# A planner that writes the instruction order of a transformer block: its model of loads, pauses, banks and delays is changed

## The chip, the cores and the metric

The kernel runs on one core of one Trainium2 chip. The metric is the device time of one execution in microseconds (us), as a median of three runs. PE is TensorE, which multiplies matrices; DVE is VectorE, ACT is ScalarE, POOL is GpSimd; SP is SyncE, which here only hands out DMA transfers. A name with q (SPq) is that engine's queue of such transfers.

## The reference, cut to what matters

One encoder block over 512 tokens of width 1024 in float32: a half-step feed-forward (FFN1), a mixer of two attention groups, and a second half-step feed-forward (FFN2), each between two RMS norms.

```python
x = x + 0.5 * post1(SwiGLU_1(pre1(x)))    # 1024 -> 2 x 2816 -> 1024
z = pre2(x) @ w_in                        # 1024 -> 1952
o_na  = neighbourhood_attention(q, k, v, rpb)     # 8 heads of 64
o_mla = latent_attention(c_q, c_kv, k_rope, ...)  # 8 heads, low rank
x = x + post2(concat(rms(o_na), rms(o_mla)) @ w_out)
x = x + 0.5 * post3(SwiGLU_2(pre3(x)))
```

A float32 product is made of three products: each operand is split into a rounded part ("hi", written by ACT) and the rest ("lo", written by DVE or POOL), and hi*hi, hi*lo and lo*hi are summed in PSUM.

## The kernel before, in words

**FFN1 and FFN2.** The hidden width of 2816 is cut into 22 chunks of 128. Every chunk has a gate and an up weight of 512 KB each. The first chunks (7 in FFN1, 3 in FFN2) are multiplied directly: 24 matmuls of 512 columns for the gate and 24 for the up weight. The others use a Strassen-Winograd scheme with 84 matmuls of 256 columns and sums on DVE and POOL. The results go to a DRAM buffer (gd); the down projection reads them back and goes over the same 22 chunks.

**The start of FFN1 (L588 to L654).** The transposed input comes in eight pieces (`load_xT`), the weights of chunks 0 and 1 as load 0 to load 3 (`load_wx`; 0 gate, 1 up of chunk 0; 2 gate, 3 up of chunk 1). There are three raw buffers: load 3 goes to the buffer of load 0 (L594), so it can start when load 0 has been split. Input rows for the norm come as four tiles of 512 KB (L646); their squares are written to PSUM banks 0 and 1 as scratch (L648), which chunk 2 needs for its sums (L388: chunk c uses banks (4+2c) and (5+2c) modulo 8). Eight small matmuls spread the norm into bank 3. `ident` (64 KB), `g_o` (4 KB) and `tokt` (128 KB) are also loaded here; the last two are used only in the mixer.

**The mixer.** `qk_pair`, `na_pair`, `k_pair`, `mla_pair`, `w_out_a` and `w_out_b` are written out in order; many of their operations read or write half the partitions of a PSUM bank.

**What sets the order.** Nothing is issued as it is written. Class `Plan` records every operation with its dependencies (`add`, `runs`, `touch`) and a reckoned duration. `place` runs a list scheduler over the five engines: at each step the engine that is free first takes the ready operation of best priority. It runs backward (which gives each operation a due time) and forward (with the due times as priority), six rounds in all (`issue`); the forward order with the shortest reckoned span is issued, sorted by reckoned start. The dependencies and semaphores on the chip follow from that order; each engine works through its list in it. Every recorded instruction is issued by L220, so the profile knows all of them by that one line, and they are told apart by engine, shape and tile (m: plain float32 tiles, memr: tiles of split operands). In `place`, an SP operation costs SP 330 ns, and its transfer is added to a line of transfers (`dma`) that can grow without bound.

Of the kernel before, what the change touches and what calls it, by code (L numbers as in the profile page):

```python
# [4 lines left out]

# [1 line left out]

# [5 lines left out]
F32 = mybir.dt.float32  # L13
# [15 lines left out]
NH = 8  # L29
TAIL = 4  # L30

# [12 lines left out]
class Plan:  # L44

    TAIL = {"ACT": 95, "DVE": 75, "POOL": 60, "PE": 176}

    def __init__(self, tc):  # L50
        self.tc, self.ops, self.maps = tc, [], {}
# [12 lines left out]
    @staticmethod  # L64
    def runs(x):

        name, ap = x.tensor.name, [list(d) for d in x.ap]
        kind = name.rsplit("_", 1)[0]
        if kind in ("h1", "h2", "gd0", "gd1"):
            n = math.prod(c for _, c in ap)  # L70
            return [((kind, 0), [(x.offset, x.offset + n)])]
        if kind not in ("m32", "memr", "psum"):
            return []
        pitch, parts = ap[0]
        p0, o = divmod(x.offset, pitch)
        runs = [(o, o + 1)]
        for step, c in sorted(ap[1:], key=lambda d: abs(d[0])):
            if step == 0 or c == 1:
                continue
            lo, hi = runs[0][0], runs[-1][1]  # L80
            if abs(step) <= hi - lo:
                a, b = (0, step * (c - 1))[:: 1 if step > 0 else -1]
                runs = [(lo + a, hi + b)]
            else:
                runs = sorted((a + step * i, b + step * i) for i in range(c) for a, b in runs)
        if kind == "psum":
            runs = sorted({(a // 512 * 512, (b + 511) // 512 * 512) for a, b in runs})
        halves = [i for i in range(2) if p0 < 64 * i + 64 and p0 + parts > 64 * i]
        return [((kind, i), runs) for i in halves]

# [18 lines left out]
    def add(self, eng, op, a, k):  # L109
        is_ap = lambda x: hasattr(x, "ap") and hasattr(x, "offset")  # L110
        outs = [x for x in (*a[:1], k.get("out"), k.get("accum_out")) if x is not None and is_ap(x)]
        ins = [x for x in (*a[1:], *(v for n, v in k.items() if n not in ("out", "accum_out"))) if is_ap(x)]
        n, deps = len(self.ops), set()
        for x in ins:
            for key, runs in self.runs(x):
                for lo, hi in runs:
                    self.touch(n, key, lo, hi, key[0] == "psum", deps)
        for x in outs:
            for key, runs in self.runs(x):
                for lo, hi in runs:  # L120
                    self.touch(n, key, lo, hi, True, deps)
        cols = max(math.prod(c for _, c in list(x.ap)[1:]) for x in outs[:1] + ins)
        kind = lambda x: x.tensor.name.rsplit("_", 1)[0]
        size = math.prod(c for _, c in list(outs[0].ap))
        big = [x for x in ins if math.prod(c for _, c in list(x.ap)[1:]) > 1]
        in_sb = sum(kind(x) != "psum" for x in big)
        tail, lock, dma = self.TAIL.get(eng, 0), False, 0
        if op == "dma_start":
            run = min(list(x.ap)[-1][1] for x in (outs[0], ins[0]))
            dma = 4 * size / (280 if run >= 512 else 230 if run >= 256 else 180 if run >= 128 else 60)  # L130
            busy, tail = (330 if eng == "SP" else 400 if eng == "ACT" else 1000), 0
        elif eng == "PE":
            busy = max(109, (cols + 32) / 2.4)
            tail += cols / 2.4 - busy
        else:
            fix, per = {"ACT": (190, 0.834) if in_sb else (132, 0.872), "DVE": (140, 1.045), "POOL": (90, 1.0)}[eng]
            if ALU.pow in a:
                fix, per = 390, 160
            elif eng == "POOL" and in_sb > 1:
                fix, per = (130, 2.2) if cols > 256 else (300, 1.2)  # L140
            fix += 90 * (AF.Exp in a) + 45 * (op == "scalar_tensor_tensor")
            if k.get("accum_out") is not None:
                fix += 195 if eng == "ACT" else 75
            busy = fix + per * cols - tail
            in_psum = sum(kind(x) == "psum" for x in big + outs)
            lock = in_sb > 1 or in_sb and (eng == "POOL" or not in_psum and eng == "DVE")
        self.ops.append((eng, op, a, k, deps, busy, tail, lock, dma))

    def place(self, prio, back):

        ops, n = self.ops, len(self.ops)
        left, after = self.left[back][:], self.after[back]
        free = dict.fromkeys(self.engines, 0.0)
        ready = {e: [] for e in free}
        soon = {e: [] for e in free}
        est, start = [0.0] * n, [0.0] * n
        lock = dma = idle = warm = 0.0
        for i in range(n):
            if not left[i]:
                heappush(soon[ops[i][0]], (0.0, prio[i], i))  # L160
        done = 0
        while done < n:
            t, e = min((max(free[e], 0.0 if ready[e] else soon[e][0][0]), e) for e in free if ready[e] or soon[e])
            ahead = 0 if e == "PE" or e == "SP" else 250
            while soon[e] and soon[e][0][0] <= t + ahead:
                s, p, i = heappop(soon[e])
                heappush(ready[e], (p, i))
            p, i = heappop(ready[e])
            _, _, _, _, deps, busy, tail, lk, xfer = ops[i]
            s = max(t, est[i])  # L170
            if lk:
                s = max(s, lock)
                lock = s + busy
            if e == "PE" and not back:
                if s > idle + 1900:
                    warm = s + 3400
                if s < warm:
                    busy *= 2 if busy > 110 else 1.2
                idle = s + busy
            free[e] = s + busy  # L180
            if xfer:
                if back:
                    x = max(s + 500, dma)
                    dma = x + xfer
                    end = dma + 1300 + 330
                else:
                    x = max(s + busy + 1300, dma)
                    dma = x + xfer
                    end = dma + 500
            else:  # L190
                end = s + busy + tail
            start[i] = s if not back else -(end if xfer else s + busy)
            done += 1
            for j in after[i]:
                est[j] = max(est[j], s + busy if ops[j][0] == e and not xfer else end + 40)
                left[j] -= 1
                if not left[j]:
                    heappush(soon[ops[j][0]], (est[j], prio[j], j))
            self.span = max(free.values())
        return start  # L200
# [28 lines left out]
def hybrid_block(ctx, tc, A, out):  # L229
# [94 lines left out]
    def load_w(src, n=1024, eng=DVE, raw=None, to=None):  # L324
        raw = fetch(src, n) if raw is None else raw
        hi, lo = to or (his.get()[:, :n], los.get()[:, :n])
        split(hi, lo, raw, eng)
        return hi, lo
# [45 lines left out]
    def ffn(w_gu, w_dn, gpost, on_tile, L, first, resid, mid_tile=None, rs=None):  # L374
# [139 lines left out]
        def down(c, n, w, first, last, hfs=(0, 1)):  # L514
            t = slice(n * P, (n + 1) * P)
            for (a, b) in ((0, 0), (0, 1), (1, 0)):
                for hf in hfs:
                    mm(bank(2 * n + hf), gT[c][a][:, t], w[b][:, hf * 512 : hf * 512 + 512],
                       first and a + b == 0, last and a == 1)
# [10 lines left out]
        for n in range(NT):  # L530
            SP.dma_start(h[n], resid(n))
        for c in range(2, NFC - TAIL):
            w = load_w(w_dn[c * P : (c + 1) * P, :])
# [3 lines left out]
        ws = []  # L537
        for c in range(NFC - TAIL, NFC):
            ws.append(load_w(w_dn[c * P : (c + 1) * P, :], to=last_w if c == NFC - 1 else None))
            load_gT(c)  # L540
        ts, sqs = cut(1024, 2), cut(512, 2, 2048)
        for n in range(NT):
            s = stat.get()
            t = ts.get()
            for hf in range(2):
                c = slice(hf * 512, hf * 512 + 512)
                for i, k in enumerate(range(NFC - TAIL, NFC)):
                    down(k, n, ws[i], False, i == TAIL - 1, (hf,))
                if hf == 0 and mid_tile:
# [650 lines left out]
```

## Time and profile before

| | us |
|---|---|
| median of 3 runs | 966.41 (966.3 to 966.68) |
| the profiled execution, its own time | 969.88 |
| its span, first to last instruction | 968.1 |
| PE busy | 948.5 (98%) |
| DVE busy | 692.8 (72%) |
| ACT busy | 464.5 (48%) |
| POOL busy | 302.0 (31%) |

Busy time is the time in which an engine has at least one instruction under way. The profiled execution is 3.5 us longer than the median run, so differences read in it are carried over to the median and not its absolute time. Its mean granted PE clock is 0.991 of full speed.

### The profile page before, as it was taken

To read this page: it belongs to the slowest core of one execution; us is meant where nothing else is said; L and a number is where in the kernel's file an instruction comes from. 1 tells how busy PE (TensorE), PEld (TensorE's weight loads), DVE (VectorE), ACT (ScalarE), POOL (GpSimd) and SP (SyncE) were. 2 spreads that over 40 slices of the span, in tenths; PEclk is the share of its full clock that TensorE was granted. 3 is DMA by queue.
4 is the path that set the end of the run, shared out by engine and by line. 5 is a ranking of instruction groups with operands and counts; after the bars stand their busy time and mean duration, and the time that the engine had idled before them with its cause. 6 is when DMAs were issued, how large, how long until landed. Compare 5 with 4: busy or idle time off the path is not lost. (4 is left out here: it accounts for less than half of the span.)

```text
span 968.1 us, 15209 instructions
## 1 busy us (share of the span) xinstructions
PE 948.5 (98%) x5878; PEld 851.8 (88%) x5878; DVE 692.8 (72%) x963; ACT 464.5 (48%) x801; POOL 302.0 (31%) x240
## 2 busy tenths in 40 slices
PE   9999999999999999999999989899999999999997
PEld 7788999999888888888988878799999999988885
DVE  4896999998522385567686587998999999742224
ACT  5553454444421362677567765764444444441211
POOL 0002767650000013222351422227777574000000
PEclk9999999999999999999999999999999999999999
DMA  9644334359743446122370112454433436753312
GB/s 288 205 156 131 128 132 145 117 155 306 225 113 96 140 159 131 62 75 45 109 165 1 66 44 88 152 183 136 151 120 110 152 127 217 250 170 109 87 44 87
DMA packets 60905, 130.11 MB, mean 134 GB/s; under 512 B 21920, under 2 KB 22816, under 8 KB 60832
## 3 DMA queue, kind: packets, MB, share of 16 engines
q1 hardware_dynamic: 59248, 126.25, 41.6%
q0 software_dynamic: 1008, 1.84, 1.1%
q10 hardware_dynamic: 576, 1.05, 0.3%
q8 instruction: 46, 0.75, 0.3%
q14 instruction: 27, 0.22, 0.1%
HBM read 109.45 MB, written 17.83 MB: 131 GB/s over the span
## 5 line engine op out<-in xcount | busy, mean ns | idle before, releaser
L220 PE MATMUL psum<-memr 128*128 128x256 f32 (+2 forms) x5520 | 921.9, 327 | 7.7 <-ACT memr L220 3.1
L220 PEld LDWEIGHTS psum<-memr 128*128 128x128 f32 x5520 | 809.6, 191 | 94.8 <-DVE memr L220 7.4
L220 DVE TENSOR_TENSOR memr<-m,memr 128x512 fp32r<-128x512 f32 (+3 forms) x310 | 353.7, 1168 | 144.1 <-ACT memr L220 143.9
L220 POOL TENSOR_TENSOR m<-m 128x512 f32<-128x512 f32 (+3 forms) x193 | 264.5, 1385 | 476.0 <-DVE m L220 368.3
L220 ACT CAST memr<-m 128x512 fp32r<-128x512 f32 (+3 forms) x318 | 259.9, 843 | 297.9 <-PE psum L220 213.5
L220 DVE TENSOR_TENSOR m<-psum,m 128x512 f32<-128x512 f32 (+3 forms) x205 | 119.9, 589 | 36.0 <-ACT m L220 21.7
L220 DVE TENSOR_TENSOR memr<-psum,memr 128x512 fp32r<-128x512 f32 (+3 forms) x116 | 68.0, 603 | 30.7 <-ACT memr L220 29.6
L220 ACT CAST memr<-psum 128x512 fp32r<-128x512 f32 (+3 forms) x124 | 62.4, 524 | 41.6 <-PE psum L220 31.8
L220 DVE TENSOR_TENSOR m<-m 128x512 f32<-128x512 f32 (+2 forms) x73 | 72.1, 999 | 6.9 <-ACT m L220 6.0
L220 PE MATMUL psum<-m 128*128 128x128 f32 (+1 forms) x358 | 58.2, 289 | 4.6 <-DVE m L220 2.8
L220 ACT ACTIVATE m<-m 128x512 f32<-128x512 f32 (+3 forms) x78 | 43.9, 564 | 33.1 <-DVE m L220 33.0
L220 PEld LDWEIGHTS psum<-m 128*128 128x128 f32 x358 | 46.6, 162 | 13.8 <-DVE m L220 3.3
L220 ACT COPY m<-psum 128x256 f32<-128x256 f32 (+2 forms) x63 | 26.1, 414 | 46.0 <-PE psum L220 33.9
L220 DVE SCALAR_TENSOR_TENSOR m<-m 128x512 f32<-128x512 f32 (+1 forms) x36 | 33.5, 966 | 4.8 <-POOL m L220 4.3
L220 ACT ACTIVATE m<-psum,m 128x512 f32<-128x512 f32 x40 | 27.4, 688 | 10.9 <-DVE m L220 10.1
L220 POOL MEMSET memr<- 128x256 f32 x8 | 2.5, 312 | 95.9 <-PE psum L220 95.9
L220 ACT ACTIVATE m<-psum 128x512 f32<-128x512 f32 (+2 forms) x27 | 14.0, 519 | 35.8 <-PE psum L220 35.8
L220 ACT ACTIVATE psum<-m 128x1024 f32<-128x1024 f32 x16 | 16.5, 1029 | 16.7 <-DVE m L220 12.1
L220 DVE TENSOR_REDUCE m<-psum 128x1 f32<-128x512 f32 x32 | 21.2, 684 | 1.0 <-PE psum L220 0.7
L220 DVE TENSOR_SCALAR m<-m 128x1 f32<-128x1 f32 (+1 forms) x36 | 6.2, 179 | 21.7 <-ACT m L220 12.2
L220 POOL TENSOR_TENSOR memr<-m,memr 128x1024 fp32r<-128x1024 f32 x8 | 19.3, 2426 | 5.1 <-ACT memr L220 5.1
L220 POOL CAST memr<-memr 64x512 fp32r<-64x512 f32 x8 | 5.8, 730 | 40.6 <-DVE memr L220 40.4
(23 smaller groups left out, 104.8 us busy)
## 6 DMA issues: line engine op xcount, KB each, us to landing
m<-in_ffn_w_gu SPq DMA_DIRECT2D x86, 512.0 KB
m<-in_ffn_w_down SPq DMA_DIRECT2D x44, 512.0 KB
gd<-m SPq DMA_DIRECT2D x44, 256.0 KB
m<-gd SPq DMA_DIRECT2D x44, 256.0 KB
m<-in_x SPq DMA_DIRECT2D x8, 512.0 KB
m<-in_w_qk SPq DMA_DIRECT2D x8, 512.0 KB
h<-m SPq DMA_DIRECT2D x8, 512.0 KB
m<-in_w_out SPq DMA_DIRECT2D x8, 512.0 KB
```

Of the source, the lines that this page charges most:

```text
L220: r = getattr(self.engines[eng], op)(*a, **k)
```

## The change

Only class `Plan` changes; what is computed, the tiles, the buffers and the recorded operations stay. Six things in it are different:

1. `runs`: a PSUM access counts for the whole bank, whichever half of the partitions it covers.
2. `add`: a matmul on plain float32 data is reckoned at twice the time.
3. `place`, look-ahead: ACT, DVE and POOL still may leave a ready operation for a better one that is not ready yet, but only when that one comes sooner than the ready one would take, and within 250 ns.
4. `place`, clock: only PE operations of over 115 ns count as activity in the planner's rule for the PE clock.
5. `place`, loads: after a transfer is handed out, SP (in the backward pass any engine) is held until no more than 4000 ns of reckoned transfers are in line.
6. Delays: the fixed 40 ns between an operation and one that depends on it on another engine becomes a delay of the engine that waits (`LAG`: ACT 60, DVE 50, POOL 85, PE 120, SP 60), and `TAIL` of POOL goes from 60 to 45.

```diff
@@ -45,7 +45,9 @@
 
-    TAIL = {"ACT": 95, "DVE": 75, "POOL": 60, "PE": 176}
+    ahead, margin = 250, 0
+    TAIL = {"ACT": 95, "DVE": 75, "POOL": 45, "PE": 176}
+    LAG = {"ACT": 60, "DVE": 50, "POOL": 85, "PE": 120, "SP": 60}
 
     def __init__(self, tc):
         self.tc, self.ops, self.maps = tc, [], {}
@@ -84,7 +86,7 @@
             else:
                 runs = sorted((a + step * i, b + step * i) for i in range(c) for a, b in runs)
         if kind == "psum":
-            runs = sorted({(a // 512 * 512, (b + 511) // 512 * 512) for a, b in runs})
+            return [((kind, 0), sorted({(a // 512 * 512, (b + 511) // 512 * 512) for a, b in runs}))]
         halves = [i for i in range(2) if p0 < 64 * i + 64 and p0 + parts > 64 * i]
         return [((kind, i), runs) for i in halves]
 
@@ -130,7 +132,7 @@
             dma = 4 * size / (280 if run >= 512 else 230 if run >= 256 else 180 if run >= 128 else 60)
             busy, tail = (330 if eng == "SP" else 400 if eng == "ACT" else 1000), 0
         elif eng == "PE":
-            busy = max(109, (cols + 32) / 2.4)
+            busy = max(109, (cols + 32) / 2.4) * (1 + (op == "matmul" and a[1].dtype == F32))
             tail += cols / 2.4 - busy
         else:
             fix, per = {"ACT": (190, 0.834) if in_sb else (132, 0.872), "DVE": (140, 1.045), "POOL": (90, 1.0)}[eng]
@@ -161,10 +163,17 @@
         done = 0
         while done < n:
             t, e = min((max(free[e], 0.0 if ready[e] else soon[e][0][0]), e) for e in free if ready[e] or soon[e])
-            ahead = 0 if e == "PE" or e == "SP" else 250
-            while soon[e] and soon[e][0][0] <= t + ahead:
+            while soon[e] and soon[e][0][0] <= t:
                 s, p, i = heappop(soon[e])
                 heappush(ready[e], (p, i))
+            p, i = ready[e][0]
+            if e != "PE" and e != "SP" and soon[e]:
+                c = min(((q, s, j) for s, q, j in soon[e] if s < t + min(ops[i][5], self.ahead)), default=(p, 0, i))
+                if c[0] < p - self.margin:
+                    p, i = c[0], c[2]
+                    soon[e].remove((c[1], p, i))
+                    heapify(soon[e])
+                    heappush(ready[e], (p, i))
             p, i = heappop(ready[e])
             _, _, _, _, deps, busy, tail, lk, xfer = ops[i]
             s = max(t, est[i])
@@ -176,23 +185,27 @@
                     warm = s + 3400
                 if s < warm:
                     busy *= 2 if busy > 110 else 1.2
-                idle = s + busy
+                if busy > 115:
+                    idle = s + busy
             free[e] = s + busy
             if xfer:
                 if back:
                     x = max(s + 500, dma)
                     dma = x + xfer
                     end = dma + 1300 + 330
+                    free[e] = max(free[e], dma - 4000)
                 else:
                     x = max(s + busy + 1300, dma)
                     dma = x + xfer
                     end = dma + 500
+                    free[e] = max(free[e], dma - 4000) if e == "SP" else free[e]
             else:
-                end = s + busy + tail
+                end = s + busy + (0 if back else tail)
             start[i] = s if not back else -(end if xfer else s + busy)
             done += 1
             for j in after[i]:
-                est[j] = max(est[j], s + busy if ops[j][0] == e and not xfer else end + 40)
+                same = ops[j][0] == e and not xfer
+                est[j] = max(est[j], s + busy if same else end + (self.LAG[e] + ops[j][6] if back else self.LAG[ops[j][0]]))
                 left[j] -= 1
                 if not left[j]:
                     heappush(soon[ops[j][0]], (est[j], prio[j], j))
```

## Rows read from the trace of the kernel before

**Rows 1.** Stretches (us from the span's start): length, busy us (x instructions) by engine, PE clock, DMA share, GB/s.
```profile
96.80:121.00 24.20, 24.20 (x204) 24.20 (x204) 24.13 (x22) 11.46 (x18) 18.91 (x12) 1.00 0.38 128
...
217.80:242.00 24.20, 24.20 (x194) 23.75 (x193) 19.96 (x30) 10.95 (x18) 0.00 (x0) 1.00 0.98 306
...
822.80:847.00 24.20, 24.20 (x180) 23.16 (x180) 18.30 (x28) 11.33 (x20) 0.00 (x0) 1.00 0.76 250
```
**Rows 2.** Stretches of the mixer, same columns (PE, PEld, DVE, ACT, POOL).
```profile
387.00:485.00 98.00, 96.43 (x554) 83.91 (x553) 63.63 (x193) 65.61 (x168) 27.89 (x39) 0.98 0.27 72
556.00:630.00 74.00, 66.49 (x408) 57.56 (x407) 60.35 (x90) 47.69 (x94) 17.29 (x21) 0.95 0.28 94
```
**Rows 3.** Timeline of PE, 5 to 28 us: start, us, what, [idle before <-releaser].
```profile
5.78 2.10 PE L220 MATMUL psum<-memr 128*128 128x512 f32 x7
...
8.09 15.31 PE L220 MATMUL psum<-memr 128*128 128x512 f32 x65 [0.22 <-DVE memr L220]
...
24.52 0.49 PE L220 MATMUL psum<-m 128*128 128x128 f32 x2 [0.45 <-DVE m L220]
26.44 15.94 PE L220 MATMUL psum<-memr 128*128 128x512 f32 x61 [1.44 <-ACT memr L220]
```
**Rows 4.** Stretches with and around the half clock.
```profile
23.00:26.50 3.50, 1.62 (x11) 1.18 (x9) 0.58 (x4) 1.48 (x4) 0.55 (x1) 1.00 0.74 291
26.50:29.90 3.40, 3.35 (x7) 2.24 (x8) 3.40 (x5) 2.88 (x4) 0.00 (x0) 0.50 0.39 82
29.90:33.00 3.10, 3.10 (x15) 2.52 (x15) 3.06 (x6) 1.68 (x2) 0.00 (x0) 1.00 0.81 268
480.40:483.90 3.50, 3.50 (x14) 2.89 (x13) 2.04 (x5) 3.08 (x5) 2.76 (x2) 0.51 0.91 337
576.00:582.90 6.90, 5.97 (x22) 5.18 (x23) 4.80 (x8) 4.04 (x10) 1.52 (x3) 0.51 0.00 0
```
**Rows 5.** Timeline of ACT, 8 to 27 us.
```profile
13.11 1.05 ACT L220 CAST memr<-m 128x1024 fp32r<-128x1024 f32 x1 [0.44 <-DMA m<-in_ffn_w_gu]
15.42 1.03 ACT L220 ACTIVATE psum<-m 128x1024 f32<-128x1024 f32 x1 [1.26 <-DMA m<-in_x]
...
22.18 1.03 ACT L220 ACTIVATE psum<-m 128x1024 f32<-128x1024 f32 x1 [1.11 <-DMA m<-in_x]
...
25.34 1.04 ACT L220 CAST memr<-m 128x1024 fp32r<-128x1024 f32 x1 [2.02 <-DMA m<-in_ffn_w_gu]
```
**Rows 6.** Timeline of SP's queue, 8 to 27 us: the hand-out, not the transfer.
```profile
8.14 2.60 SPq L220 DMA_DIRECT2D m<-in_x  x4
10.78 0.59 SPq L220 DMA_DIRECT2D m<-in_ident  x1
...
11.89 0.52 SPq L220 DMA_DIRECT2D m<-in_tokt  x1
13.16 4.84 SPq L220 DMA_DIRECT2D m<-in_ffn_w_gu  x3
```
**Rows 7.** Timeline of DVE, 7 to 9 us.
```profile
8.01 0.96 DVE L220 TENSOR_TENSOR memr<-m,memr 128x768 fp32r<-128x768 f32 x1
```
**Rows 8.** Timeline, 391 to 395 us: two halves of one bank.
```profile
391.80 1.20 ACT L220 ACTIVATE memr<-psum 64x512 fp32r<-64x512 f32 x2 [6.44 <-PE psum L220]
...
393.03 1.41 DVE L220 SCALAR_TENSOR_TENSOR memr<-psum,memr 64x512 fp32r<-64x512 f32 x2 [6.95 <-ACT memr L220]
```
**Rows 9.** The chain that ended last, first pieces: start, us, what.
```profile
605.42 0.07 issue
...
606.95 0.03 issue
```
**Rows 10.** Timeline of PE, 570 to 590 us.
```profile
573.24 0.35 PE L220 MATMUL psum<-memr 128*128 128x256 f32 x1 [0.32 <-DVE m L220]
574.47 1.09 PE L220 MATMUL psum<-memr 128*128 128x256 f32 x7 [0.87 <-DVE memr L220]
576.93 1.12 PE L220 MATMUL psum<-m 128*128 128x128 f32 x4 [1.38 <-ACT m L220]
```

More of the change, by code (lines that the diff above doesn't have):

```diff
@@ L3 @@
 from contextlib import ExitStack
-from heapq import heappop, heappush
+from heapq import heapify, heappop, heappush
 import numpy as np
```

## The prediction, made blind

> **What bounds the kernel now.** I read the page's busy shares first, then the stretches of the span, then, where PE stands still, the timelines of PE, ACT and SP's queue. PE is busy 948.5 of 968.1 us. In the long part of both FFNs nothing can be won: in a Winograd stretch PE is busy all of its 24.20 us, and at the turn to the down projection too, even with the DMA share at 0.98 [rows 1]. The order of instructions can only change the places where PE stands or runs at half clock. These are few. At the start, PE ends 65 matmuls at 23.40, does some small ones, and goes on at 26.44 [rows 3]; in the 3.50 us from 23.0 it is busy 1.62, and in the next 3.40 us the granted clock is 0.50 and 7 matmuls start where the following 3.10 us hold 15 [rows 4]. In the mixer PE is idle 1.57 us between 387 and 485 and 7.51 us between 556 and 630 [rows 2], and two further stretches, of 3.50 and 6.90 us, are granted 0.51 [rows 4]. The rest of the idle time is the tail after the last matmul, whose order is forced.
>
> **The start: load 3.** The wait before 26.44 is for a cast on ACT [rows 3], and that cast, at 25.34, waited 2.02 us for a weight [rows 5]. It is load 3, the up weight of chunk 1: by then 7 + 65 = 72 matmuls have been done [rows 3], which is three weights of 24. Its buffer is that of load 0, which DVE has read at 8.01 + 0.96 = 8.97 [rows 7]. It could have been handed out there, but SP handed out the four input tiles at 8.14 to 10.74, then ident, g_o and tokt, and the first weight only at 13.16 [rows 6]. The tiles land 2.25 us apart ((22.18 - 15.42) / 3) [rows 5], and load 3 stands behind them.
>
> Why the planner did that follows from the code. Its SP needs 330 ns for an issue and its line of transfers may be of any length. After one small, eight xT pieces and load 2 it is free at 3.3 us of its own time; load 3 is not ready, the input tiles are, and it hands out all that is ready, tokt too, which only the mixer wants. With the hold (part 5 of the change), the same transfers are reckoned by the code's rates: four pieces for chunk 0, 2 x 0.57 + 2 x 1.40 = 3.9 us; eight xT, 7.5; load 2, 1.9; with 1.6 for the first start, the line ends near 14.9, so SP is held to about 10.9. By then load 3 is ready (8.97 on the chip), and the due time decides. Load 3 is due for PE at 23.40, less cast and split. The input tiles are due only when chunk 2 needs banks 0 and 1, 24 matmuls later. So I expect load 3 before at least most of the tiles.
>
> What it gives: behind load 2, which had landed by 13.11 [rows 5], with up to three tiles in front, load 3 lands by 13.11 + 3 x 2.25 + 2.25 = 22.1 at the slowest, and the cast of 1.04 is over at 23.2, in time for 23.40. With all four in front it is as before. So three may pass it and the gain still holds. PE then goes on without the pause: it saves 3.50 - 1.62 = 1.88 us of idle time. In the half-clock stretch one matmul takes 15.31 / 65 = 0.236 us at full clock, so 3.40 us hold 14.4, of which 7 were started: 7.4 x 0.236 = 1.75 us. Together 3.6 us.
>
> What is late next: the tiles move back by one load. The last one began to be squared at 22.18 and is now at most 2.25 later, 24.4, squared by 25.5; chunk 2 needs its banks after 24 x 0.236 = 5.7 us more, at 29.1. The gate weight of chunk 2 uses load 3's buffer again. Behind the tiles it lands by 24.4 + 2.25 = 26.7, cast by 27.7: 1.4 us to spare. If two other weights go in front, it comes up to 4.5 us later and 3.1 of the 3.6 us are lost. The small loads g_o and tokt may stay early; they cost little in either place.
>
> **The delays and the look-ahead.** LAG changes each hand-over by 10 (DVE) to 80 ns (PE). The chain of waits shows 0.07 us from DVE to POOL and 0.03 back to DVE [rows 9]: 85 for POOL is nearer than 40, 50 for DVE is not. No operation becomes longer or shorter by this; only ranks change between operations that lie within some 100 ns. The shorter look-ahead saves at most 0.25 us of an engine's time at each place, on ACT, DVE and POOL, which between 556 and 630 have 13.7, 26.3 and 56.7 us free [rows 2]; what it costs or gains is seen only at the PE waits counted above. Small matmuls of plain data are doubled and the clock rule is sharpened: this moves ranks at the start and in the mixer, nothing else.
>
> **The banks.** In qk_pair ACT writes both halves of a pair in 1.20 us from 391.80, so the first half is ready near 392.4, yet DVE, which had been idle 6.95 us, begins at 393.03, after the second [rows 8]. The chip's program already treats the bank as one, and the old planner did not know it. So I cost this edit at nothing. The Trainium skill, in PSUM — Partial Sum Buffer, section "PSUM bank collisions raise a hardware error", says that two engines may use different quadrants of one bank at the same time; by it the planner would now give up an overlap of 0.6 us in each of the 8 such places, 4.8 us of ACT and DVE time. The row says that this overlap is not there to be given up.
>
> **The mixer, all edits together.** No row shows the new order, so I bound it. What can be won there is 1.57 + 7.51 us of idle time and half of what ran at half clock, (3.50 + 5.97) x 0.49 = 4.6: 13.7 us. I bound the gain by the largest knot: the waits of 0.32, 0.87 and 1.38 us before 577 [rows 10], the 5.97 x 0.49 = 2.9 after them and one more wait of the longest kind, together 6.8. I bound the loss by one more knot of this size, 2.57 + 2.9 = 5.5. The last waits, after 605, hang on a chain through DVE, POOL and ACT whose operations stay as they are, so I take a tenth of the 13.7: 1.3 us won. It is a choice near the middle, on the side of delays that agree better with the rows for POOL.
>
> **The sum.** -3.6 - 1.3 = -4.9 us. Against the profiled execution that is 969.9 to 965.0; carried to the median, 966.4 - 4.9 = 961.5 us.
>
> **Rivals.**
>
> (1) Load 3 goes first, but the mixer gives the gain back (a loss of 1.7 to 5.5): 964.5 to 968.3, about 966.5. Speaking for it: every operation of the mixer may change its place, and the knots there are a few tenths of a us wide.
>
> (2) The hold does not move load 3: due times put the tiles in front because the four squares have to run one after the other on ACT. Then only the mixer's small changes are left: 966.4, or 965.1 with the tenth. Against it: the tiles' need comes 5.7 us after load 3's.
>
> (3) Slower, by the hold itself. The chip's SP isn't held, only the planner's; where many transfers are in line, at the turn from gate and up to down, weights, stores and reads of gd can be put in an order in which a weight stands behind others, as load 3 did. Both FFNs have this turn [rows 1], with a DMA share of 0.98 in the first, and PE has no idle time there now. One such weight costs what it cost at the start, 3.6 us; two, with the start mended, 966.4 - 3.6 + 7.2 - 1.3 = 968.7. It decides from two late weights on, or from one where the start stays as it is (970.0). Against it: in the turn in FFN2 the DMA share is 0.76 and DVE has 24.20 - 18.30 = 5.9 us free [rows 1], which leaves room for a load that comes late.
>
> (4) Slower, by the clock. The planner counts a pause of PE only above a fixed length of its own, but the clock fell at 576 after three waits of which the longest was 1.38 us [rows 10, 4]. An order that trades long waits for several short ones can look better to the planner and bring two more such stretches: 966.4 - 3.6 + 2 x 5.5 = 973.8; one gives 968.3. The Trainium skill, in TensorE: Matmul & The Clock Gate, section "A second HAM failure mode: psum-queue depth-cycling", tells of frequent short idle times between groups of matmuls that make the clock go back and forth; the trace agrees at 576.
>
> **How the numbers follow.** About 0.2% (1.9 us) can be told from no change. Forecast, load 3 first and the mixer within +6.8 won and 1.7 lost: 0.60, 956.0 to 964.5. Rival 1: 0.13. Rival 2: 0.10, of which 0.03 with a mixer gain above the bound. Rival 3: 0.09; rival 4: 0.08. Faster: 0.60 + 0.03 = 0.63. Same: 0.13 + 0.07 = 0.20. Slower: 0.17. The range goes from 955.5 to 969.5; it leaves out the dearer part of rivals 3 and 4 and a gain in the mixer above 6 us.
>
> **What would show it.** Right: in SP's queue a weight stands before the third or fourth input tile; the cast of load 3 is over before 23.4; PE has no wait of over 1 us before 30 us and no half-clock stretch there. Wrong: the first weight after the tiles again, or a new wait for a weight at about 30, 240 or 820 us. For the mixer: idle time of PE from 387 to 485 and 556 to 630 against 1.57 and 7.51 us, and the number of half-clock stretches there (now two). The forecast would be wrong above all if the mixer's knots, which I can't follow, move by more than the start gives.

## The result, and the profile after

The changed kernel takes 961.62 us as a median (959.81 to 962.65, 5 runs). The kernel before, run beside it, takes 966.41 (965.72 to 969.19, 5 runs). The ratio is 0.9944, 95% interval 0.9925 to 0.9963. It is faster by 4.8 us as the medians have it, and by 5.4 us as the ratio has it. In a second comparison (e5 below) it took 960.84, ratio 0.9935 [0.9919, 0.9951].

The profiled execution of the changed kernel took 962.65 us, its span is 960.8 us; the one of before took 969.88, with a span of 968.1. Head of the page, changed kernel (busy us, share of the span, instructions):

```profile
span 960.8 us, 15214 instructions
...
PE 944.1 (98%) x5878; PEld 850.9 (89%) x5878; DVE 681.5 (71%) x963; ACT 463.6 (48%) x801; POOL 303.7 (32%) x240
```

The engines do the same work; PE loses 4.4 us of busy time (948.5 before) and 2.9 us of idle time. The start first. Timeline of SP's queue, changed kernel (start, us, what; the hand-out and not the transfer):

```profile
7.13 2.43 SPq L233 DMA_DIRECT2D m<-in_ffn_w_gu  x2
9.61 1.31 SPq L233 DMA_DIRECT2D m<-in_x  x2
...
11.59 1.19 SPq L233 DMA_DIRECT2D m<-in_x  x2
17.21 1.28 SPq L233 DMA_DIRECT2D m<-in_ffn_w_gu  x3
```

Load 2 and load 3 now go out one behind the other, ahead of all four input tiles; before, four tiles stood between them [rows 6]. Timeline of ACT, changed kernel:

```profile
13.10 1.05 ACT L233 CAST memr<-m 128x1024 fp32r<-128x1024 f32 x1 [0.45 <-DMA m<-in_ffn_w_gu]
14.88 1.05 ACT L233 CAST memr<-m 128x1024 fp32r<-128x1024 f32 x1 [0.73 <-DMA m<-in_ffn_w_gu]
...
24.09 1.03 ACT L233 ACTIVATE psum<-m 128x1024 f32<-128x1024 f32 x1 [1.13 <-DMA m<-in_x]
...
26.25 1.05 ACT L233 CAST memr<-m 128x1024 fp32r<-128x1024 f32 x1 [1.01 <-DMA m<-in_ffn_w_gu]
```

The cast of load 3 begins at 14.88 instead of 25.34 [rows 5], the square of the last tile at 24.09 instead of 22.18, and the chunk-2 gate weight is cast by 27.30. Timeline of PE, changed kernel:

```profile
22.48 1.88 PE L233 MATMUL psum<-memr 128*128 128x512 f32 x7
...
26.41 1.88 PE L233 MATMUL psum<-memr 128*128 128x512 f32 x7
...
28.26 17.05 PE L233 MATMUL psum<-memr 128*128 128x512 f32 x74
```

No line from 22 us on has a wait in brackets, where before had two [rows 3]. Stretches, changed kernel (columns as in rows 1; the first two answer to rows 4, the turns to rows 1):

```profile
23.00:26.50 3.50, 3.50 (x19) 2.89 (x18) 0.88 (x4) 1.40 (x3) 1.10 (x2) 1.00 1.01 364
26.50:29.90 3.40, 3.40 (x18) 2.82 (x17) 1.92 (x2) 2.16 (x3) 0.00 (x0) 1.00 0.34 105
217.80:242.00 24.20, 24.20 (x179) 23.09 (x178) 18.15 (x28) 11.37 (x19) 0.00 (x0) 1.00 0.85 272
387.00:485.00 98.00, 95.84 (x551) 84.81 (x551) 69.80 (x198) 67.12 (x172) 32.31 (x44) 0.97 0.32 82
475.40:482.20 6.80, 6.12 (x19) 4.61 (x18) 5.51 (x8) 2.52 (x5) 4.34 (x4) 0.50 0.38 135
556.00:630.00 74.00, 68.46 (x446) 60.32 (x445) 64.89 (x94) 51.04 (x95) 16.78 (x18) 0.98 0.33 108
822.80:847.00 24.20, 24.20 (x151) 21.88 (x150) 17.48 (x26) 13.50 (x22) 0.00 (x0) 1.00 0.73 230
```

The half clock at 26.5 is gone, PE is busy all through both turns, and in the mixer the idle time is 2.16 and 5.54 us (1.57 and 7.51 before [rows 2]).

These fixed windows hold different work in the two kernels, since everything has moved. So I cut the span where PE has started the same number of matmuls. Then a stretch holds the same number of PE instructions in every kernel, and its length says what changed. They are nearly the same instructions: the start and D hold the same shapes in all kernels, while at the other cuts the orders differ and a few matmuls are exchanged (more on this below). Stretches cut in this way, kernel before (up to the first Winograd matmul of FFN1, then A, B, C and D, one after the other in the mixer):

```profile
0.00:85.74 85.74, 82.53 (x355) 67.57 (x356) 63.13 (x88) 41.19 (x55) 3.70 (x9) 0.98 0.63 199
...
403.97:473.96 69.99, 69.09 (x417) 61.34 (x416) 46.36 (x149) 47.80 (x135) 18.89 (x30) 1.00 0.24 57
473.96:551.48 77.52, 77.22 (x415) 64.30 (x415) 55.89 (x102) 54.87 (x109) 27.20 (x28) 0.98 0.34 86
551.48:604.57 53.09, 49.73 (x277) 42.13 (x276) 39.00 (x68) 33.32 (x75) 15.86 (x18) 0.94 0.24 80
604.57:627.75 23.18, 19.04 (x139) 17.13 (x138) 21.74 (x26) 16.18 (x25) 5.48 (x4) 1.00 0.47 159
```

The same stretches, changed kernel:

```profile
0.00:81.87 81.87, 80.37 (x355) 65.87 (x356) 63.51 (x88) 40.79 (x55) 3.70 (x9) 1.00 0.67 208
...
400.50:468.67 68.17, 68.17 (x417) 62.05 (x416) 48.35 (x147) 48.32 (x133) 18.41 (x28) 1.00 0.29 69
468.67:547.26 78.59, 77.52 (x415) 65.43 (x414) 55.60 (x103) 52.92 (x110) 26.00 (x28) 0.96 0.25 66
547.26:597.05 49.79, 47.69 (x277) 39.77 (x276) 38.75 (x68) 33.31 (x74) 19.26 (x19) 1.00 0.29 96
597.05:620.26 23.21, 19.77 (x139) 18.38 (x138) 21.63 (x26) 16.35 (x27) 5.68 (x4) 0.93 0.46 159
```

The start gives 85.74 - 81.87 = 3.87 us, stretch A 1.82, stretch C 3.30; B takes 1.07 back, with 6.8 us of half clock in it where before had 3.5 [rows 4]; D is the same. The early mixer (to 403.97 and 400.50) is 0.4 us longer, the rest within 0.2. Together 3.87 + 1.82 + 3.30 - 1.07 - 0.03 - 0.4 - 0.2 = 7.3 us, the difference of the spans. So this pair of executions differs by more than the medians (4.8), and the mixer gives about as much as the start.

How much do the exchanged matmuls blur this? Groups of PE by shape in C, kernel before (551.48 to 604.57), then changed (547.26 to 597.05); columns: shape and count, busy us and mean ns, idle us before. A group takes in a matmul that reaches over the first cut.

```profile
L220 PE MATMUL psum<-memr 128*128 128x512 f32 x121 | 34.8, 418 | 0.1
L220 PE MATMUL psum<-m 128*128 128x2 f32 x12 | 1.6, 239 | 0.0
...
L233 PE MATMUL psum<-memr 128*128 128x512 f32 x125 | 33.7, 403 | 0.0
L233 PE MATMUL psum<-m 128*128 128x2 f32 x8 | 0.9, 240 | 0.0
```

C of the changed kernel has four matmuls of 512 columns in place of four of 2 columns. In the trace of e5 (400 to 620 us), matmuls start 0.23 us apart with 512 columns, 0.19 with 416, 0.12 with 256 and 0.11 with fewer (medians). By these paces I estimate that C of the changed kernel holds 0.5 us more work than before, A 0.4 us more and B 0.8 us less. Like for like, A gives about 2.2 us and C 3.8, and B takes 1.9 back; their sum hardly changes.

### The profile page after: what moved, and what is told of

Its sections match the earlier page's. It is cut to its first block, busy times and chain, and to the rows that moved or that the text cites. A ratio compares the mean times of both kernels' runs of the same rounds, so it can differ in the third digit from the quotient of the medians.

```text
span 960.8 us, 15214 instructions
## 1 busy us (share of the span) xinstructions
PE 944.1 (98%) x5878; PEld 850.9 (89%) x5878; DVE 681.5 (71%) x963; ACT 463.6 (48%) x801; POOL 303.7 (32%) x240
## 5 line engine op out<-in xcount | busy, mean ns | idle before, releaser
L233 DVE TENSOR_TENSOR memr<-m,memr 128x512 fp32r<-128x512 f32 (+3 forms) x310 | 348.6, 1146 | 137.6 <-ACT memr L233 137.2
L233 DVE TENSOR_TENSOR m<-m 128x512 f32<-128x512 f32 (+2 forms) x73 | 64.6, 892 | 9.8 <-ACT m L233 8.5
```

The lines of the kernel that those rows point to most:

```text
L233: r = getattr(self.engines[eng], op)(*a, **k)
```

## The experiments

The code records the same operations in two planners, each with its own set of parts switched on. What the first planner reckons to start before 200 us goes out in its order, the rest in the second's order. The parts are named `bank` (1), `dbl` (2), `look` (3), `clock` (4), `hold` (5) and `lag` (6); `ALL` is all six. Each short diff is against the changed kernel, after this common one:

```diff
-    plan = Plan(tc)
-    plan.issue()
+    plans = [Plan(tc, parts) for parts in (ALL, ALL)]
+    starts = [p.issue() for p in plans]      # reckoned starts; cut at 200 us
```

Times are medians in us with range and number of runs, the ratio is to the kernel before on the same chip: 967.21 (965.43 to 969.02, 12) beside e1 to e4, 967.34 (964.66 to 970.44, 17) beside e5 to e8, 967.32 (965.39 to 970.32, 24) beside e9 to e12.

| kernel | median (range, runs) | ratio [95%] |
|---|---|---|
| e1 start changed, rest as before | 963.9 (963.03 to 964.86, 6) | 0.9964 [0.9952, 0.9976] |
| e2 start as before, rest changed | 962.96 (961.95 to 965.94, 6) | 0.9959 [0.9943, 0.9974] |
| e3 hold alone | 963.36 (962.44 to 965.28, 6) | 0.9961 [0.9945, 0.9976] |
| e4 all but the hold | 963.6 (963.31 to 964.65, 5) | 0.9963 [0.995, 0.9976] |
| e5 changed kernel again | 960.84 (960.32 to 961.45, 6) | 0.9935 [0.9919, 0.9951] |
| e6 three tiles before load 3 | 962.79 (961.39 to 964.09, 6) | 0.9955 [0.9939, 0.9971] |
| e7 four tiles before load 3 | 963.85 (962.43 to 965.41, 12) | 0.9966 [0.9956, 0.9977] |
| e8 start changed, then delays alone | 962.62 (962.0 to 963.93, 6) | 0.9955 [0.9939, 0.997] |
| e9 start changed, then banks alone | 964.62 (963.45 to 966.02, 11) | 0.997 [0.9959, 0.9982] |
| e10 start changed, then all but banks | 964.08 (961.27 to 965.15, 11) | 0.9957 [0.9944, 0.9971] |
| e11 start changed, then look-ahead alone | 963.55 (962.87 to 965.59, 8) | 0.9959 [0.9945, 0.9973] |
| e12 changed, pow counted against DVE | 958.55 (957.37 to 961.36, 6) | 0.991 [0.9892, 0.9929] |

The lengths of the five stretches in each profiled execution, cut as above and taken from the rows of the same view; the granted clock stands in brackets where it is below 1.00:

| kernel | start | A | B | C | D |
|---|---|---|---|---|---|
| before | 85.74 (0.98) | 69.99 | 77.52 (0.98) | 53.09 (0.94) | 23.18 |
| changed | 81.87 | 68.17 | 78.59 (0.96) | 49.79 | 23.21 (0.93) |
| e5 | 82.12 | 68.10 | 76.31 | 49.76 | 23.24 (0.93) |
| e1 | 82.62 | 70.18 | 76.74 | 51.76 (0.97) | 23.20 (0.93) |
| e3 | 81.66 | 69.97 | 76.70 | 51.96 (0.97) | 23.17 (0.93) |
| e2 | 84.13 | 68.08 | 75.87 | 49.89 | 23.22 (0.93) |
| e4 | 84.07 | 68.12 | 76.16 | 49.84 | 24.14 (0.86) |
| e6 | 83.34 | 68.09 | 78.10 (0.96) | 49.77 | 23.23 (0.93) |
| e7 | 84.67 | 68.10 | 75.65 | 50.06 | 24.05 (0.86) |
| e8 | 82.45 | 69.01 | 76.93 | 52.19 (0.97) | 23.19 (0.93) |
| e9 | 81.62 | 69.19 | 77.58 | 51.74 (0.97) | 23.19 (0.93) |
| e10 | 82.08 | 68.94 | 79.93 (0.96) | 49.79 | 24.16 (0.86) |
| e11 | 82.21 | 69.79 | 75.75 | 51.85 | 23.19 (0.93) |
| e12 | 81.50 | 67.90 | 76.45 | 50.05 | 20.72 |

Read it by columns. A repeats to 0.1 us among kernels with the same mixer order (68.08 to 68.17 for six of them), so one trace is enough there. C repeats to 0.3, and the start to 1.1 (81.50 to 82.62 where load 3 comes first or second). B does not: with the changed mixer order (changed, e2, e4 to e7) it takes 75.65 to 76.31 us at a clock of 1.00, and 78.10 and 78.59 at 0.96.

### e1 and e2: the start and the rest, each alone

```diff
-    plans = [Plan(tc, parts) for parts in (ALL, ALL)]
+    plans = [Plan(tc, parts) for parts in (ALL, set())]      # e1
+    plans = [Plan(tc, parts) for parts in (set(), ALL)]      # e2
```

> Both planners run; what the changed one starts in its first 200 us is issued in its order, everything after that in the order of the kernel before. Theory A (the gain is the start, the mixer adds about 1 us): 966.4 - 3.6 = 962.8 us, PE without a wait of over 1 us before 30 us, and the mixer's idle time near the 1.57 + 7.51 us of before. Theory B (the gain is the new mixer order): 965.5 to 966.5 us.

> The mirror image: the first 200 us in the order of the kernel before, the rest in that of the changed one. Theory A: 961.6 + 3.6 = 965.2 us, with the wait for load 3 and the half clock near 26 us back. Theory B: 962 us.

Each half is faster than before by itself: e1 by 3.5 us (0.36%), e2 by 4.0 (0.41%), as the ratios have it, with intervals that exclude no change. A theory in which the start carries all, or the mixer gives back, is out: the changed order from the mixer on is worth about as much as the start. Stretches of e2, cut as above:

```profile
0.00:84.13 84.13, 80.69 (x355) 65.82 (x356) 63.09 (x88) 41.25 (x55) 3.71 (x9) 1.00 0.64 203
...
546.71:596.60 49.89, 47.78 (x278) 39.76 (x276) 38.85 (x68) 33.43 (x74) 19.26 (x19) 1.00 0.29 96
```

The old start order has its wait here (PE stands 0.77 us ahead of 25.45 and 0.53 us ahead of 27.07) and yet the clock stays at 1.00: the half clock of before at 26.5 did not come. The stretch is 2.0 us longer than that of e5 (84.13 against 82.12), and the half clock came on top in one execution and not in another.

### e3 and e4: the hold alone, and all but the hold

```diff
-    plans = [Plan(tc, parts) for parts in (ALL, ALL)]
+    plans = [Plan(tc, {"hold"})]             # e3
+    plans = [Plan(tc, ALL - {"hold"})]       # e4
```

> The planner of before with part 5 alone (the hold on loads). Theory A: load 3 in front of at least one tile, no wait at 25 us, 3.6 us won at the start; the mixer is ordered anew, which I can bound only by 3 us to either side: 960 to 966, most likely 962.8. Theory B: the start is no faster than before, or the time stays at 966.

> The changed planner without part 5. Theory A: the tiles in front of load 3 again, the wait near 25 us and the half clock after it are back: 965.2 us, within 3 us for the mixer. Theory B (the delays, banks and clock rule bring the gain): 961 to 963 us.

The hold alone moves load 3: its stretch to the first Winograd matmul is 81.66 us, as short as the changed kernel's, with one tile in front of load 3. Timeline of SP's queue, e3:

```profile
7.82 0.68 SPq L240 DMA_DIRECT2D m<-in_x  x1
9.03 0.33 SPq L240 DMA_DIRECT2D m<-in_ffn_w_gu  x1
9.40 0.57 SPq L240 DMA_DIRECT2D m<-in_x  x1
```

Without it (e4) the start is that of before, four tiles in front, and 84.07 us. In the mixer it is the other way round: e3 has the A and C of before (69.97, 51.96), e4 those of the changed kernel (68.12, 49.84). Each of the two is ordered by one planner from end to end. So the hold is the start's part, and the mixer's gain comes from the other five.

### e5 to e7: how many tiles may pass load 3

```diff
# e5: the changed kernel as it is
-                    free[e] = max(free[e], dma - 4000) if e == "SP" else free[e]
+                    free[e] = max(free[e], dma - 12000) if e == "SP" else free[e]      # e6, first planner
+                    free[e] = max(free[e], dma - 14000) if e == "SP" else free[e]      # e7, first planner
```

The same number stands in the line for the backward pass. The mixer's order is that of the changed kernel in all three.

> The changed kernel once more, timed beside the next three. Theory A (start and mixer add up): e1 and e2 together were 3.5 + 4.0 us below the kernel before, so 7 us below it, near 960. Theory C (the two overlap, for the start's gain is smaller than e1 alone shows): 5 us below, near 961.6.

> The hold at 12000 ns in place of 4000 for the first 200 us, which puts load 3 behind three of the four tiles; the rest in the order of the changed kernel. The working before the result (three may pass, the cast is over by 23.2): same as the changed kernel within 1 us, no PE wait over 1 us before 30 us. Rival (any tile in front costs its 2.25 us): PE waits at 23 us, 3 us slower than the changed kernel.

> The hold at 14000 ns for the first 200 us: load 3 behind all four tiles and ident, but in front of g_o and tokt; the rest in the order of the changed kernel. By the working before the result the cast starts near 24 to 24.5: PE waits 1 to 2 us there, and with a half clock after it 1 to 3.5 us slower than the changed kernel. Rival (the place of load 3 is not the cause): no slower.

Four tiles in front cost 963.85 - 960.84 = 3.0 us, three cost 1.95 (the intervals of e5 and e6 overlap a little). Timeline of PE, e6:

```profile
24.36 0.71 PE L241 MATMUL psum<-memr 128*128 128x512 f32 x2
25.49 2.37 PE L241 MATMUL psum<-memr 128*128 128x512 f32 x9 [0.41 <-DVE memr L241]
```

With three tiles in front, PE waits again, briefly, for load 3. Timeline of ACT, e6:

```profile
14.19 1.05 ACT L241 CAST memr<-m 128x1024 fp32r<-128x1024 f32 x1 [1.31 <-DMA m<-in_ffn_w_gu]
...
23.12 1.05 ACT L241 CAST memr<-m 128x1024 fp32r<-128x1024 f32 x1 [0.93 <-DMA m<-in_ffn_w_gu]
```

The cast ends at 24.17 where I had worked out 23.2, and the split by DVE comes behind it. The 1 us is that of load 2, whose cast begins at 14.19 here and began at 13.11 before [rows 5]; from there to load 3's cast it takes 8.93 us, where the working had 4 x 2.25 = 9.0. Timeline of PE, e7:

```profile
26.40 0.49 PE L241 MATMUL psum<-m 128*128 128x128 f32 x2 [0.85 <-DVE m L241]
...
27.59 6.66 PE L241 MATMUL psum<-memr 128*128 128x512 f32 x28 [0.23 <-DVE memr L241]
```

The start's stretch follows: 82.12, 83.34 and 84.67.

### e8 to e11: which part of the mixer's order

```diff
-    plans = [Plan(tc, parts) for parts in (ALL, ALL)]
+    plans = [Plan(tc, parts) for parts in (ALL, {"lag"})]            # e8
+    plans = [Plan(tc, parts) for parts in (ALL, {"bank"})]           # e9
+    plans = [Plan(tc, parts) for parts in (ALL, ALL - {"bank"})]     # e10
+    plans = [Plan(tc, parts) for parts in (ALL, {"look"})]           # e11
```

> The first 200 us of the changed kernel, the rest ordered by the planner of before with part 6 alone (LAG and TAIL). Theory D (the delays brought the mixer's gain, since they move most of its order): like the changed kernel, 960.5 to 962. Rival (the bank and look-ahead parts did): like e1, 963 to 964.

> The first 200 us of the changed kernel, the rest ordered by the planner of before with part 1 alone (a PSUM access counts for the whole bank). Theory E (the bank part brought the mixer's gain: the planner now knows the waits that the program has anyway): no half clock near 572 us, which all four profiles of the old mixer order show and no profile of the new one, and 961 us. Theory F (no part alone brings it): half clock near 572, 963 to 964, like e1.

> The mirror image: after the first 200 us all parts but part 1. Theory E: half clock near 572 back, 963 to 964. Theory F: like the changed kernel, 960.5 to 962.

> After the first 200 us part 3 alone (the shorter look-ahead). Theory G (the look-ahead brought it, by not leaving ACT and DVE idle for 250 ns): no half clock near 572 and 961 us. Theories E and F: like e1, 963 to 964.

By the medians none of the four reaches e5: they stand 1.8 to 3.8 us above it, but the intervals of e8, e10 and e11 overlap that of e5. So the medians can't order the four, nor rule out by themselves that one part made the mixer's gain. The stretches can, in part.

**Stretch A** splits. The old order takes 69.97 to 70.18 us, the new one 68.08 to 68.17. Delays alone give 69.01, banks alone 69.19, look-ahead alone 69.79, all but banks 68.94. So the delays are worth about 1.0 us and the banks 0.8, and they add up. (By the shapes, A of e8, e9 and e10 holds 0.1 us more work than the old order's and that of the new order 0.4 more, so these gains are a little understated.) What the banks' edit does is seen in the first of the four qk_pairs, which lies just ahead of A. Timeline of ACT and DVE, e9:

```profile
387.44 0.59 ACT L242 ACTIVATE memr<-psum 64x512 fp32r<-64x512 f32 x1 [7.57 <-PE psum L242]
387.93 1.03 ACT L242 CAST memr<-m 128x1024 fp32r<-128x1024 f32 x1
388.99 0.59 ACT L242 ACTIVATE memr<-psum 64x512 fp32r<-64x512 f32 x1
...
388.06 0.68 DVE L242 SCALAR_TENSOR_TENSOR memr<-psum,memr 64x512 fp32r<-64x512 f32 x1 [7.47 <-ACT memr L242]
```

ACT writes one half, DVE takes it at once, and ACT does a cast meanwhile and the other half afterwards. Before, ACT wrote both halves in a row and DVE began behind the second [rows 8]; e8, with the delays alone, does that still. DVE now begins 0.62 us after ACT's start instead of 1.23. The old planner did not know that the second half would be waited for; the new one does, and puts other work there. That this is what shortens A is not shown: in the three later qk_pairs, which lie in A, e8 has the halves apart as e9 has (ACT at 402.89 and 404.44, DVE between them at 403.50). PE stands 0.90 us in A before, 0.68 in e8, 0.69 in e9 and not at all in the changed kernel; the rest of the gain was not followed.

The Trainium skill (PSUM — Partial Sum Buffer, "PSUM bank collisions raise a hardware error") says that two engines may use different quadrants of one bank at once. On the halves shown here, neither kernel has ACT and DVE at work in one bank at the same time in any of the four pairs.

**Stretch C** doesn't split by its length. The old order takes 51.76 and 51.96 us at a clock of 0.97 (53.09 at 0.94), the new one 49.76 to 50.06 at 1.00. Delays, banks and look-ahead alone leave 52.19, 51.74 and 51.85; all but banks has the whole gain, 49.79. So the banks aren't needed, and no part that was run alone has the gain. These lengths are not quite like for like: e11's C holds about 0.5 us more work than the new order's (four matmuls of 512 columns in place of four of 128), and that of e8 has a half clock in it. Timeline of PE in the knot, e11:

```profile
569.65 0.36 PE L242 MATMUL psum<-memr 128*128 128x256 f32 x1 [0.36 <-DVE m L242]
570.88 1.10 PE L242 MATMUL psum<-memr 128*128 128x256 f32 x7 [0.87 <-DVE memr L242]
573.30 0.66 PE L242 MATMUL psum<-m 128*128 128x128 f32 x4 [1.32 <-ACT m L242]
```

The changed kernel in the same place:

```profile
569.69 0.36 PE L233 MATMUL psum<-memr 128*128 128x256 f32 x1 [0.42 <-DVE m L233]
...
570.91 1.09 PE L233 MATMUL psum<-memr 128*128 128x256 f32 x7 [0.65 <-DVE memr L233]
572.32 0.66 PE L233 MATMUL psum<-m 128*128 128x128 f32 x4 [0.31 <-ACT m L233]
```

The waits of 0.36 + 0.87 + 1.32 become 0.42 + 0.65 + 0.31, 1.2 us less. The delays alone bring 1.0 us of that. Timeline of PE, e8, the third of these places:

```profile
572.07 1.54 PE L241 MATMUL psum<-m 128*128 128x128 f32 x6 [0.32 <-ACT m L241]
```

The waits of e8 are 0.34 + 0.87 + 0.32. Yet 3.4 us at half clock begin there, at 572.0, and C stays long. Whether they belong to e8's order or to that one execution can't be told from one trace. What it takes beside the delays, of look-ahead, doubling and clock rule, was not settled; the last two were never run alone.

e10's median stays above e5 (964.08) although its C is as good: its profiled execution has a half clock in B and D (0.96, 0.86), and its 11 executions go from 961.27 us at a mean clock of 0.997 to 965.15 at 0.990.

### e12: the knot after 600

The largest knot left is 2.19 and 0.96 us of waiting near 604 in the changed kernel. The second of these waits hangs on a chain through POOL's pow (pow from 602.71 to 604.17, DVE from 604.21 to 605.49, PE at 605.64). The planner reckons that long operations on SBUF, DVE's and POOL's with two large inputs above all, run one at a time (a lock); pow, on one column, is not among them. I put it under the lock, in the second planner:

```diff
+            lock = lock or ALU.pow in a
```

> The changed planner with one thing more after the first 200 us: it counts POOL's pow as an operation that DVE's two-input operations on plain memory keep waiting, as the trace shows (1.40 us beside such an operation, 0.55 alone). If the waits near 601 and 604 us, which both orders have, come from pow in the wrong place: 1 to 2 us below the changed kernel, about 959.5. If they are the chain's own length: like the changed kernel, 960.8 to 961.6.

It takes 958.55 us, 8.8 below before, and 2.3 below e5 (960.84), though these last two intervals still overlap. Timeline of PE, e12:

```profile
600.99 6.38 PE L242 MATMUL psum<-memr 128*128 128x256 f32 x51 [2.56 <-DVE memr L242]
607.21 1.04 PE L242 MATMUL psum<-m 128*128 128x128 f32 x8
```

The changed kernel in the same place:

```profile
603.82 0.85 PE L233 MATMUL psum<-memr 128*128 128x256 f32 x5 [2.19 <-DVE memr L233]
605.64 1.94 PE L233 MATMUL psum<-m 128*128 128x128 f32 x8 [0.96 <-DVE m L233]
```

One wait of 2.56 us is left of the two: 51 matmuls now stand ahead of the second, where there were 5. D falls from 23.2 to 20.72, while start, A, B and C stay within 0.7 us of e5's. The operation itself did not become shorter (groups of POOL, 32 pow: mean 755 ns, where e5 has 746). So the gain comes from another order, not from a shorter pow.

## Why the prediction came out right

961.5 us was forecast, faster, and 961.62 was measured. The total is closer than its terms were, and that is luck: two of them missed to opposite sides.

**The wait for load 3: right.** It vanished as forecast, by the hold alone (e3). Without a half clock it is worth about 2.0 us of the start's stretch (84.13 and 84.07 in e2 and e4 against 82.12 in e5), where 1.88 was forecast. The chunk-2 gate weight was the next one due, as said; it was cast by 27.30 where 27.7 was reckoned, and nothing waited.

**"Three may pass it and the gain still holds": slightly too generous.** The cast with three in front ends 1 us later than my bound, since load 2, from which I had counted, landed 1.1 us later than in before, and I had left out DVE's split behind the cast. The start's stretch of e6 is 1.2 us longer than that of e5; a wait of 0.41 us of it is seen at load 3, and the stretch spreads by 1.1 us even among kernels in which load 3 goes early.

**The half clock at the start, 1.75 us: right in the profiled pair, wrong when carried to the median.** It is in the profiled execution of before, but with the same start order, e2 and e4 have 84.13 and 84.07 us at 1.00. It belongs to an execution, not to the order: in that of before, load 3 was cast at 25.34 and PE's longest wait was 1.44 us [rows 3, 5]; in e2 and e4 it was cast at 24.70 and 24.69, with longest waits of 0.77 and 0.53 us. I subtracted it from a median in which it may not be. In company, the start is worth 2.1 us (e2 against e5) to 3.0 (e7), not 3.6; e1 alone measured 3.5.

**The mixer, -1.3: the term that was mis-sized.** e2 measured -4.0, e4 -3.6, within the bound of 6.8 but three times the choice. Two steps lay behind it. The banks' edit was costed at nothing, from the true reading that the program serves the bank as one; but a planner that knows this orders around it, 0.8 us in A. Of the delays I wrote that "only ranks change"; that is what they do, and it is worth 1.0 us in A. (One reading there was crossed: between 556 and 630 DVE has 13.7 us free and ACT 26.3 [rows 2]; no term hung on it.) For C, I bounded the gain by the knot before 577, and there it came: 1.2 us of waits, and no half clock in any of eight traces whose planner had everything but perhaps the hold or the banks, against at least one in each of the three with the old order (0.94, 0.97, 0.97). The half clock does not go with these waits in every trace, though: e11 has the old waits and no half clock in C, e8 shorter ones and a half clock. The last waits, after 605, stayed as forecast (D 23.18 and 23.21), but not because the chain left no choice: in e12 another order took 2.5 us out of D. The start's shortfall and the mixer's surplus cancelled.

**The rivals.** Rival 1 (the mixer gives it back) and rival 2 (the hold does not move load 3) are refuted by e2 and e3. Rival 3 did not happen: both turns have PE busy for all of 24.20 us. Rival 4 happened in part: a new wait of 1.09 us at 397.92 and a longer half clock in B (6.8 us, 475.4 to 482.2) are in the changed kernel's trace, but e5, the same program, has B at 1.00 and 76.31 us. The number of half-clock stretches in the mixer is two in that trace (6.8 us at 475.4, 3.4 us at 605.1), as before, and one in e5's.

**What stays open.** Which combination makes C shorter; how the delays and the banks shorten A; and why the gains of e1 and e2 add to 7.5 us where the two together gave 5.4 and 6.3 (all by the ratios). Intervals of 1 to 2 us to either side of each and the clock's play in B can hold that difference; it was not shown that they do.

## What to carry to other kernels

Cut two traces at equal counts of the busiest engine's instructions, not at equal times: in stretch A, such lengths repeated to 0.1 us here and took a gain apart that medians with intervals of 2 us could not. Count the matmuls by shape as well, since a few exchanged at a cut blurred lengths by up to 0.8 us. A list scheduler can gain from a true model of what will be waited for even where the chip does nothing new, because it fills the time with other work, as in e9's first qk_pair. And before a half-clock stretch is put into a sum, see whether it is there in a second execution of the same order.

## What the runs showed of the hardware

The mean granted clock differs between executions of one program: 0.990 to 0.997 over 11 of e10, with times from 965.15 to 961.27 us. The same order of the start has 3.4 us at half clock behind the waits near 25 us in before (the longest 1.44 us) and none in e2 and e4 (the longest 0.77 and 0.53 us).

A half-clock stretch can be free. Stretch D takes 23.18 us at a clock of 1.00 and 23.17 to 23.24 at 0.93, since PE waits there for a chain through other engines; at 0.86 it takes 24.05 to 24.16. In B, where PE is the bound, 0.96 costs about 2 us (78.10 and 78.59 against 75.65 to 76.31).

Loads that are handed out in the same order don't land at the same times: load 3 was cast 1.78 us after load 2 in the changed kernel (13.10 and 14.88) and 2.98 us after it in e1 (13.78 and 16.76), each as soon as it had landed. With the start order of before, load 2 was cast at 13.11 in that trace, at 14.60 in e2 and at 14.84 in e4.
